# Raw weight slots by quarters, handed on in a circle, and a new order of products and sums in the MLP of a hybrid encoder layer

## The chip, the cores and the metric

The kernel runs on one NeuronCore of a Trainium2 chip. The metric is the device time of one execution in microseconds (us), here the median of three runs. In the profile PE is the matmul engine (its weight loads are PEld), DVE is VectorE, ACT is ScalarE, POOL is GpSimd and SP is the engine that issues most of the transfers.

## What is computed

One layer of a streaming encoder on 512 tokens of width 2048, all in float32: a token mixer, a residual and a layer norm, then the part that the change touches, an MLP with 8192 hidden units.

```python
mix = token_mixer(h, ...)
x = layer_norm(ALPHA * x + g1 * mix, ln1_g, ln1_b)
h = x * (1.0 + sc2) + sh2
ff = jnp.square(jax.nn.relu(h @ w_ff1)) @ w_ff2      # 2048 -> 8192 -> 2048
x = layer_norm(ALPHA * x + g2 * ff, ln2_g, ln2_b)
```

## The kernel before

**Three matmuls for one.** A float32 operand is split into a high part and a low part in the rounded matmul type: `split(h, l, src)` has ACT copy `src` into `h` (L57, the tiles `wh`) and DVE subtract `h` from `src` into `l` (L60, the tiles `wl`). A product is then h·h + l·h + h·l, three matmuls. Most raw weights are loaded by `load` (L127) into the pool `rawp`, four slots of 1 MB under the name `raw`.

**Seven products for eight.** In most of the MLP a unit multiplies a block of weights, cut into quarters a11, a21, a12, a22, with quarters of the activations by Strassen's scheme in Winograd's form. The function `strassen` (L1179) makes seven products of one quarter or one sum of quarters each, named p1 to p7, and eight matrix additions on the weights: s1 = a21 + a22, s2 = s1 + a11, then in place a11 = a11 + a21 and s2 = s2 + a12; each is done in two halves `c` of 128 x 1024 elements. The tiles of s1 and s2 come from four slots (`st` in the first matrix, `s` in the second). Each product is likewise run in two halves: split half c of the quarter into a `wh` and a `wl` (three buffers of each), then the matmuls. The order is p1 (a11), p2 (a12), p6 (s2), p7 (a11 + a21), p5 (s1), p4 (a22), p3 (s2 + a12). Three PSUM areas x, z, v collect the products, and `read` takes each result out of PSUM.

**First matrix.** Block 0 of w_ff1 is done with plain products; then `ff1_unit(b)` runs for blocks 1 to 15, 48 matmuls of 256 columns in a product (L202 to L204). A unit loads four tiles of 1 MB: `lo[c]` holds a11 beside a21, `hi[c]` a12 beside a22. The sums of s are formed behind the two halves of p2 (`late=True`). The inputs t3, n2, n1 and t4 are made on DVE and ACT just before unit 1, from tiles `st` that are read from `hx_d` in runs of 1 KB. What `read` takes out becomes four quarters of the hidden activations (ACT: ReLU and square; DVE: adds). For blocks 0 to 13 seven pieces (three quarters, four sums) are split into tiles `hc` (two slots) and stored to `hc_d`, 512 KB each in runs of 4 KB (`put`, L1090). They stand in a list, `waiting`, and `spread()` runs one of them after each product. Blocks 14 and 15 are stored to `h_d`.

**Second matrix.** `ff2_unit(e, cp, ...)` runs for seven row blocks e and two column pairs cp, 14 units, 24 matmuls of 512 columns in a product (L1374 to L1376). Again four loads of 1 MB. The activations are read back as `hin` (1 MB for each of the seven pieces, in the order of the list `ORDER`), the next e's while the current one's second unit runs. Here the sums of s are formed behind p1. `read` adds each result to `ffa` on DVE; for e > 0 the quadrant (0, 0) goes through an ACT copy `c` and an accumulating transfer that POOL issues. Beside the units run background jobs: `base` (tiles `y`, `lng`, `lnb`) and the gate row g2 (`araw`, `adaz`, and matmuls with `ones` on L1335). The last block e = 7 is done with plain products, followed by the last layer norm.

**What sets the order.** A planner puts each engine's instructions in one fixed order before the run, by its own estimate of durations and by priorities; loads of weights (`w_load`, +2500) and splits and sums (`w_split`, +4000) go ahead of most else. On the chip each engine then works through its list in order, so an instruction that waits holds up all that stand behind it, on SP too. A load is held on SP until its slot's last reader is done.

## Time and profile before

| | us |
|---|---|
| runs | 2266.93, 2272.72, 2273.12; median 2272.72 |
| profiled execution, its own time | 2262.95 |
| its span, first to last instruction | 2261.2 |
| PE busy | 2159.0 (95%) |
| DVE busy | 1873.2 (83%) |
| ACT busy | 1092.9 (48%) |
| granted TensorE clock, mean | 0.987 of full |

The profiled execution's own time lies 1.75 us above its span. Busy time of PE counts pipelined matmuls whose ends are modelled, so a busy PE is not a PE at its peak. In the span the first matrix's units run from 971.8 to 1609.4 us and the second's from 1611.0 to 2160.2 us.

### The profile page before, as it was taken

To read this page: it belongs to the slowest core of one execution; us is meant where nothing else is said; L and a number is where in the kernel's file an instruction comes from. 1 tells how busy PE (TensorE), PEld (TensorE's weight loads), DVE (VectorE), ACT (ScalarE), POOL (GpSimd) and SP (SyncE) were. 2 spreads that over 40 slices of the span, in tenths; PEclk is the share of its full clock that TensorE was granted. 3 is DMA by queue.
4 is the path that set the end of the run, shared out by engine and by line. 5 is a ranking of instruction groups with operands and counts; after the bars stand their busy time and mean duration, and the time that the engine had idled before them with its cause. 6 is when DMAs were issued, how large, how long until landed. Compare 5 with 4: busy or idle time off the path is not lost.

```text
span 2261.2 us, 30621 instructions
## 1 busy us (share of the span) xinstructions
PE 2159.0 (95%) x11947; PEld 1849.2 (82%) x11947; DVE 1873.2 (83%) x2520; ACT 1092.9 (48%) x1570; POOL 44.6 (2%) x55
## 2 busy tenths in 40 slices
PE   6999999988899999999999999999999999999997
PEld 4778887866676787899999999999888887878886
DVE  7886889998776776798778778778699989998788
ACT  3323434458855223666555555555444444444432
POOL 0000000000000000000000000000000000000000
PEclk9999999999999999999999999999999999999999
DMA  8877553264224576745654544553788988796562
GB/s 320 320 292 278 182 216 135 96 208 154 79 84 172 208 282 264 242 142 205 212 187 178 199 183 176 197 187 140 289 303 281 335 276 290 236 343 226 146 235 90
DMA packets 129626, 485.59 MB, mean 215 GB/s; under 512 B 15556, under 2 KB 38468, under 8 KB 88264
## 3 DMA queue, kind: packets, MB, share of 16 engines
q1 hardware_dynamic: 122952, 471.04, 56.9%
q0 software_dynamic: 6528, 12.58, 3.3%
q8 instruction: 94, 1.54, 0.3%
q14 instruction: 52, 0.43, 0.1%
HBM read 392.35 MB, written 78.64 MB: 208 GB/s over the span
## 4 chain that ended last, share of the span: by engine, by line
PE 44%; DVE 32%; DMA 15%; ACT 5%; issue 4%; DVEq 0%; SPq 0%; ACTq 0%
DMA raw<-in_wff_dram 11%; DVE wl L60 10%; PE two L1375 4%; PE two L1376 4%; PE two L1374 4%; DVE st L60 4%; PE mm L210 4%; PE mm L209 4%; PE mm L208 4%; PE mm L197 4%; PE mm L198 4%; PE mm L196 4%; DVE ffa L60 2%; DVE adaz L63 2%; DVE hc L60 2%
## 5 line engine op out<-in xcount | busy, mean ns | idle before, releaser
L57 ACT ACTIVATE wh<-raw 128x1024 fp32r<-128x1024 f32 x332 | 349.5, 1057 | 427.4 <-PE two L1376 137.9
L60 DVE TENSOR_TENSOR wl<-raw,wh 128x1024 fp32r<-128x1024 f32 x332 | 403.1, 1220 | 69.4 <-ACT wh L57 68.9
L1375 PE MATMUL two<-wl,hin 128*128 128x512 f32 x784 | 307.8, 393 | 3.3 <-DVE wl L60 3.0
L1374 PE MATMUL two<-wh,hin 128*128 128x512 f32 x784 | 307.1, 392 | 3.8 <-ACT wh L57 2.1
L1376 PE MATMUL two<-wh,hin 128*128 128x512 f32 x784 | 306.1, 390 | 0.0
L196 PE MATMUL mm<-acts,wh 128*128 128x512 f32 (+1 forms) x568 | 225.5, 400 | 7.3 <-ACT ve L57 3.8
L203 PE MATMUL mm<-acts,wl 128*128 128x256 f32 x720 | 209.4, 291 | 18.4 <-DVE wl L60 18.2
L197 PE MATMUL mm<-acts,wl 128*128 128x512 f32 (+1 forms) x568 | 223.6, 394 | 1.9 <-DVE wl L60 1.7
L198 PE MATMUL mm<-acts,wh 128*128 128x512 f32 (+1 forms) x568 | 223.6, 395 | 0.0
L63 DVE SCALAR_TENSOR_TENSOR adaz<-raw,cols,adaz 128x1024 f32<-128x1024 f32 (+2 forms) x180 | 198.3, 1112 | 17.5 <-DMA raw<-in_adaR_dram 13.4
L202 PE MATMUL mm<-acts,wh 128*128 128x256 f32 x720 | 206.1, 286 | 1.3 <-ACT ev L57 1.3
L204 PE MATMUL mm<-acts,wh 128*128 128x256 f32 x720 | 206.0, 286 | 0.0
L203 PE MATMUL mm<-tx,wl 128*128 128x256 f32 x720 | 203.8, 283 | 0.0
L204 PE MATMUL mm<-tx,wh 128*128 128x256 f32 x720 | 203.3, 282 | 0.0
L202 PE MATMUL mm<-tx,wh 128*128 128x256 f32 x720 | 201.9, 280 | 0.0
L1375 PEld LDWEIGHTS two<-wl,hin 128*128 128x128 f32 x784 | 147.6, 188 | 40.3 <-DVE wl L60 9.2
L1374 PEld LDWEIGHTS two<-wh,hin 128*128 128x128 f32 x784 | 147.5, 188 | 36.0 <-ACT wh L57 3.0
L209 PE MATMUL mm<-wl,acts 128*128 128x512 f32 x448 | 175.0, 391 | 1.2 <-DVE wl L60 1.0
L210 PE MATMUL mm<-wh,acts 128*128 128x512 f32 x448 | 174.7, 390 | 0.0
L208 PE MATMUL mm<-wh,acts 128*128 128x512 f32 x448 | 173.6, 391 | 0.2 <-DVE r L60 0.2
L1376 PEld LDWEIGHTS two<-wh,hin 128*128 128x128 f32 x784 | 147.6, 188 | 30.4
L203 PEld LDWEIGHTS mm<-acts,wl 128*128 128x128 f32 x720 | 140.6, 195 | 24.4 <-DVE wl L60 24.4
(316 smaller groups left out, 4539.1 us busy)
## 6 DMA issues: line engine op xcount, KB each, us to landing
raw<-in_wff_dram SPq DMA_DIRECT2D x128, 1024.0 KB, 6.4
hc_d<-hc SPq DMA_DIRECT2D x98, 512.0 KB, 3.8
hin<-hc_d SPq DMA_DIRECT2D x49, 1024.0 KB, 9.0
raw<-in_adaR_dram SPq DMA_DIRECT2D x48, 1024.0 KB, 5.1
raw<-in_adaS_dram SPq DMA_DIRECT2D x32, 1024.0 KB, 9.0
raw<-in_wo_dram SPq DMA_DIRECT2D x16, 1024.0 KB, 5.0
araw<-in_adaR_dram SPq DMA_DIRECT2D x16, 1024.0 KB, 6.3
raw<-in_wconv_dram SPq DMA_DIRECT2D x12, 1024.0 KB, 4.8
```

The costliest lines, as they stand in the source:

```text
L57: S.activation(o, i, f, **kw)
L60: V.tensor_tensor(o, a, b, op=op)
L196: T.matmul(ps, wh, xh, start=start, stop=False)
L197: T.matmul(ps, wl, xh, start=False, stop=False)
L198: T.matmul(ps, wh, xl, start=False, stop=stop)
L202: T.matmul(ps, wh, xh, start=start, stop=False, skip_group_check=True)
L203: T.matmul(ps, wl, xh, start=False, stop=False, skip_group_check=True)
L204: T.matmul(ps, wh, xl, start=False, stop=stop, skip_group_check=True)
L209: T.matmul(ps, xh, wl, start=False, stop=False)
L1374: T.matmul(ps[:, t], xh, h[:, k], start=first, stop=False, skip_group_check=True)
L1375: T.matmul(ps[:, t], xh, l[:, k], start=False, stop=False, skip_group_check=True)
L1376: T.matmul(ps[:, t], xl, h[:, k], start=False, stop=last, skip_group_check=True)
```

## The change

Two things change in the MLP's units.

Loads: a unit's weights come as eight loads of 512 KB, one for each quarter and half, in the order a22, a21, a11, a12, into eight half slots (four tiles, allocated once for all units). From one unit to the next the slots are handed on: a22 takes the slot that a21 had, a21 that of a11, a11 that of a12, a12 that of a22. In the first matrix a quarter is a slice of 256 columns, so its runs are 1 KB; in the second they are 4 KB.

Order: s1 is formed before anything else, then come p1 (a11), a21 = a21 + a11 in place, p7 (a21), s2 = s1 + a11, p6 (s2), s2 = s2 + a12, p2 (a12), p5 (s1), p4 (a22), p3 (s2). `ORDER` follows, and `spread` takes two pieces after p1, one after p7, none after p6 and p2, one after p5 and p4 and two after p3.

```diff
-    ORDER = ("b11", "b21", "n2", "t3", "n1", "t4", "b22")
+    ORDER = ("b11", "t3", "n2", "b21", "n1", "t4", "b22")
...
-    waiting = []
-
-    def spread(n=1):
+
+    waiting, PIECES = [], dict(p1=2, p7=1, p6=0, p2=0, p5=1, p4=1, p3=2)
+
+    def spread(n):
...
-    def strassen(halves, tile4, widths, operate, read, late=False):
...
-        def product(ps, name, x, start, stop, behind=None):
...
+    slot8, place = [], {}
+
+    def raw_quarters(sources):
+
+        if not slot8:
+            for _ in range(4):
+                r = rawp.tile([128, 2, 1024], F32, name="raw", bufs=4)
+                slot8.extend([r[:, 0], r[:, 1]])
+            place.update(a11=0, a21=1, a12=2, a22=3)
+        else:
+            place.update(a22=place["a21"], a21=place["a11"], a11=place["a12"], a12=place["a22"])
+        w4 = [{}, {}]
+        for name in ("a22", "a21", "a11", "a12"):
+            for c in range(2):
+                src = sources[name][c]
+                w4[c][name] = slot8[2 * place[name] + c].rearrange("p (k n) -> p k n", k=src.shape[1])
+                with prio("w_load"):
+                    nc.sync.dma_start(w4[c][name], src)
+        return w4
+
+    def strassen(w4, tile4, widths, operate, read):
+
+
+        def sums(name, x, y, new=False):
+            for c in range(2):
+                with prio("w_split"):
+                    if new:
+                        w4[c][name] = tile4()
+                    tt(w4[c][name], w4[c][x], w4[c][y], OP.add)
+
+        def product(ps, name, x, start, stop):
...
         x, z, v = yield
+        sums("s1", "a21", "a22", True)
         product(x, "a11", "b11", True, False)
-        if not late:
-            form(0)
-            form(1)
+        sums("a21", "a21", "a11")
         read("p1", x)
-        product(v, "a12", "b21", True, True, form if late else None)
-        for c in range(2):
-            with prio("w_split"):
-                tt(w4[c]["a11"], w4[c]["a11"], w4[c]["a21"], OP.add)
+        product(z, "a21", "t3", True, False)
+        sums("s2", "s1", "a11", True)
+        read("p7", z)
+        product(x, "s2", "n2", False, False)
+        sums("s2", "s2", "a12")
+        read("p6", x)
+        product(v, "a12", "b21", True, True)
         read("p2", v)
-        product(x, "s2", "n2", False, False)
...
         product(x, "s1", "n1", False, False)
         read("p5", x)
         product(z, "a22", "t4", False, True)
...
     def ff1_unit(b):
...
+        w4 = raw_quarters({f"a{i + 1}{j + 1}": [A["wff1"][b][2 * j + c][:, :, 256 * i:256 * i + 256] for c in range(2)]
+                           for i in range(2) for j in range(2)})
...
-            spread()
+            spread(PIECES[name])
...
     def ff2_unit(e, cp, h_in, h_next):
...
+        w4 = raw_quarters({f"a{i + 1}{j + 1}": [A["wff2"][e][2 * cp + i][c][:, 2 * j:2 * j + 2] for c in range(2)]
+                           for i in range(2) for j in range(2)})
```

## Rows read from the trace of the kernel before

**Rows 1.** The page's part 1 (busy us of each engine, its share of the span, instructions) and, from its part 5, the groups of the split's ScalarE step (line, operation, tiles, shapes, count; busy us and mean ns of one; idle us before and what ended it).

```profile
PE 2159.0 (95%) x11947; PEld 1849.2 (82%) x11947; DVE 1873.2 (83%) x2520; ACT 1092.9 (48%) x1570; POOL 44.6 (2%) x55
...
L57 ACT ACTIVATE wh<-raw 128x1024 fp32r<-128x1024 f32 x332 | 349.5, 1057 | 427.4 <-PE two L1376 137.9
```

**Rows 2.** Busy time by stretch of the span: the 15 units of the first MLP matrix, the 14 units of the second, and the first 12 of those 14. Columns: stretch and its length, busy us (and instructions) of PE, its weight loads, DVE, ACT, POOL; granted TensorE clock, mean busy share of the DMA engines, GB/s.

```profile
971.80:1609.40 637.60, 618.16 (x5040) 611.68 (x5040) 508.48 (x531) 367.95 (x479) 0.00 (x0) 0.99 0.52 187
...
1611.00:2160.20 549.20, 543.78 (x2361) 443.08 (x2362) 497.70 (x455) 242.33 (x234) 29.89 (x25) 1.00 0.80 274
...
1611.00:2081.80 470.80, 465.38 (x2021) 379.21 (x2021) 430.95 (x394) 204.65 (x197) 25.09 (x21) 1.00 0.85 293
```

**Rows 3.** The columns of rows 2, one row for a unit of the first matrix (units 1, 4, 5 and 12 of 15). A row counts an instruction at an edge twice, so 338 stands for 336 matmuls.

```profile
971.80:1013.60 41.80, 40.81 (x337) 40.53 (x337) 37.71 (x39) 26.05 (x37) 0.00 (x0) 1.00 0.45 152
...
1096.80:1144.00 47.20, 43.81 (x339) 43.20 (x338) 37.36 (x40) 26.88 (x36) 0.00 (x0) 0.93 0.49 179
1144.00:1184.30 40.30, 40.30 (x338) 40.30 (x338) 33.16 (x36) 24.16 (x32) 0.00 (x0) 1.00 0.54 197
...
1438.10:1485.40 47.30, 43.70 (x339) 43.09 (x338) 36.24 (x39) 26.68 (x36) 0.00 (x0) 0.93 0.45 167
```

**Rows 4.** The columns of rows 2, one row for a unit of the second matrix (the first, third, fifth, seventh, eighth and tenth of 14).

```profile
1611.00:1654.70 43.70, 40.77 (x169) 32.76 (x169) 35.97 (x35) 17.16 (x17) 0.00 (x0) 0.96 0.85 319
...
1693.10:1731.20 38.10, 38.10 (x169) 31.54 (x169) 36.26 (x32) 17.61 (x17) 2.53 (x2) 1.00 0.94 325
...
1769.60:1808.10 38.50, 38.48 (x169) 31.38 (x168) 38.20 (x35) 16.71 (x16) 2.40 (x2) 1.00 0.95 324
...
1846.50:1886.50 40.00, 38.84 (x169) 31.31 (x169) 35.01 (x36) 16.70 (x16) 2.40 (x2) 1.00 0.80 245
1886.50:1926.80 40.30, 40.15 (x173) 32.22 (x172) 36.40 (x34) 17.72 (x17) 3.35 (x3) 1.00 0.88 307
...
1965.00:2005.40 40.40, 39.32 (x169) 31.17 (x168) 37.07 (x33) 16.70 (x16) 2.40 (x2) 1.00 0.81 277
```

**Rows 5.** Who waited for whom between 971.8 and 1609.4 us. Columns: waiting engine, tile and line, what it waited for, us in total, times, longest us.

```profile
DVE st L60 <- DMA raw<-in_wff_dram: 81.5, 28, 5.1
...
ACT hc L57 <- DMA hc_d<-hc: 41.0, 32, 4.8
...
PE mm L203 <- DVE wl L60: 18.2, 25, 2.8
```

**Rows 6.** DVE in order of time, from unit 7 of the first matrix to unit 8 (which begins at 1267.2 us). Columns: start us, us, engine, line, operation, tiles, shapes; in brackets the idle time before and what ended it.

```profile
1252.05 1.23 DVE L60 TENSOR_TENSOR st<-raw 128x1024 f32<-128x1024 f32 x1 [3.32 <-DMA raw<-in_wff_dram]
...
1254.45 2.35 DVE L60 TENSOR_TENSOR wl<-raw,wh 128x1024 fp32r<-128x1024 f32 x2
...
1265.06 1.23 DVE L60 TENSOR_TENSOR st<-raw 128x1024 f32<-128x1024 f32 x1 [3.45 <-DMA raw<-in_wff_dram]
```

**Rows 7.** SP's transfers in order of time, same stretch (x2: two issued in the time given).

```profile
1242.52 2.67 SPq L127 DMA_DIRECT2D raw<-in_wff_dram  x2
...
1255.69 1.47 SPq L127 DMA_DIRECT2D raw<-in_wff_dram  x2
```

**Rows 8.** Groups of DVE instructions between 971.8 and 1609.4 us. Columns: line, operation, tiles, shapes and count; busy us and mean ns of one; idle us before them and what ended it.

```profile
L60 DVE TENSOR_TENSOR wl<-raw,wh 128x1024 fp32r<-128x1024 f32 x120 | 145.4, 1219 | 7.8 <-ACT wh L57 7.8
L60 DVE TENSOR_TENSOR wl<-st,wh 128x1024 fp32r<-128x1024 f32 x90 | 109.9, 1222 | 24.5 <-ACT wh L57 24.5
L60 DVE TENSOR_TENSOR st<-st,raw 128x1024 f32<-128x1024 f32 x60 | 73.2, 1221 | 0.5
L60 DVE TENSOR_TENSOR hc<-ev,hc 128x512 fp32r<-128x512 f32 x98 | 66.1, 687 | 12.5 <-ACT hc L57 12.5
L60 DVE TENSOR_TENSOR raw<-raw 128x1024 f32<-128x1024 f32 x30 | 36.6, 1220 | 0.0
L60 DVE TENSOR_TENSOR st<-raw 128x1024 f32<-128x1024 f32 x29 | 35.5, 1226 | 81.5 <-DMA raw<-in_wff_dram 81.5
```

**Rows 9.** Transfers by tiles over the whole span. Columns: tiles, issuing queue, operation and count, KB each, median us from issue to landing.

```profile
raw<-in_wff_dram SPq DMA_DIRECT2D x128, 1024.0 KB, 6.4
hc_d<-hc SPq DMA_DIRECT2D x98, 512.0 KB, 3.8
...
st<-hx_d SPq DMA_DIRECT2D x8, 512.0 KB, 5.9
```

**Rows 10.** Groups of PE instructions between 1611 and 2160.2 us (columns as in rows 8).

```profile
L1335 PE MATMUL two<-adaz,ones 128*128 128x512 f32 x8 | 3.8, 592 | 0.0
```

**Rows 11.** PE in order of time at the start of the first unit of the second matrix, two of the starts after an idle time.

```profile
1624.86 0.50 PE L1374 MATMUL two<-wh,hin 128*128 128x512 f32 x1 [2.12 <-ACT wh L57]
1626.16 0.50 PE L1375 MATMUL two<-wl,hin 128*128 128x512 f32 x1 [0.81 <-DVE wl L60]
```

**Rows 12.** DVE in order of time in the same stretch as rows 11.

```profile
1613.62 0.43 DVE L67 TENSOR_SCALAR lng<-lng 128x512 f32<-128x512 f32 x1 [1.90 <-DMA lng<-in_ln1g_dram]
...
1616.35 1.22 DVE L60 TENSOR_TENSOR s<-raw 128x1024 f32<-128x1024 f32 x1
...
1624.89 2.35 DVE L60 TENSOR_TENSOR wl<-s,wh 128x1024 fp32r<-128x1024 f32 x2
```

**Rows 13.** DVE in order of time in the tenth unit of the second matrix.

```profile
1994.61 1.22 DVE L60 TENSOR_TENSOR s<-raw 128x1024 f32<-128x1024 f32 x1 [2.84 <-DMA raw<-in_wff_dram]
```

**Rows 14.** DVE in order of time in the seventh unit of the second matrix.

```profile
1860.18 0.69 DVE L60 TENSOR_TENSOR y<-y,lng 128x512 f32<-128x512 f32 x1 [2.37 <-DMA y<-xn_d]
```

More of the change, by code (lines that the diff above doesn't have):

```diff
@@ L1177, in trunk_kernel @@
             parts(t4, a)
-    def strassen(halves, tile4, widths, operate, read, late=False):
-        w4 = [dict(zip(("a11", "a21", "a12", "a22"), h)) for h in halves]
-        def form(c):
-            with prio("w_split"):
-                tt(new_s(c, "s1"), w4[c]["a21"], w4[c]["a22"], OP.add)
-                tt(new_s(c, "s2"), w4[c]["s1"], w4[c]["a11"], OP.add)
-        def new_s(c, name):
-            w4[c][name] = tile4()
-            return w4[c][name]
-        def product(ps, name, x, start, stop, behind=None):
+    slot8, place = [], {}
[23 more added lines that the diff above has]
+        def product(ps, name, x, start, stop):
             for c in range(2):
@@ L1198, in product @@
                     split(h, l, w4[c][name])
-                if behind is not None:
-                    behind(c)
                 operate(ps, h, l, x, c, start and c == 0, stop and c == 1)
         x, z, v = yield
+        sums("s1", "a21", "a22", True)
         product(x, "a11", "b11", True, False)
-        if not late:
-            form(0)
-            form(1)
+        sums("a21", "a21", "a11")
         read("p1", x)
-        product(v, "a12", "b21", True, True, form if late else None)
-        for c in range(2):
-            with prio("w_split"):
-                tt(w4[c]["a11"], w4[c]["a11"], w4[c]["a21"], OP.add)
-        read("p2", v)
-        product(x, "s2", "n2", False, False)
-        for c in range(2):
-            with prio("w_split"):
-                tt(w4[c]["s2"], w4[c]["s2"], w4[c]["a12"], OP.add)
-        read("p6", x)
-        product(z, "a11", "t3", True, False)
-        read("p7", z)
+        product(z, "a21", "t3", True, False)
[5 more added lines that the diff above has]
+        product(v, "a12", "b21", True, True)
+        read("p2", v)
         product(x, "s1", "n1", False, False)
@@ L1235, in ff1_unit @@
     def ff1_unit(b):
-        lo, hi = [None] * 2, [None] * 2
-        for c in range(2):
-            lo[c] = load(A["wff1"][b][c], [128, 4, 512])
-            hi[c] = load(A["wff1"][b][2 + c], [128, 4, 512])
-        halves = [(lo[c][:, :, 0:256], lo[c][:, :, 256:512], hi[c][:, :, 0:256], hi[c][:, :, 256:512])
-                  for c in range(2)]
+        w4 = raw_quarters({f"a{i + 1}{j + 1}": [A["wff1"][b][2 * j + c][:, :, 256 * i:256 * i + 256] for c in range(2)]
+                           for i in range(2) for j in range(2)})
         inputs = dict(b11=b11, b21=b21, n2=n2, t3=t3, n1=n1, t4=t4, b22=b22)
@@ L1283, in read @@
                 sums_done(b, [part[q] for q in QUARTERS])
-            spread()
-        run(strassen(halves, st_tile, [128, 4, 256], operate, read, True), (bank(), bank(), bank("sa")))
+            spread(PIECES[name])
+        run(strassen(w4, st_tile, [128, 4, 256], operate, read), (bank(), bank(), bank("sa")))
     for b in range(1, 16):
@@ L1357, in ff2_unit @@
     def ff2_unit(e, cp, h_in, h_next):
-        wa, wb = [None] * 2, [None] * 2
-        for c in range(2):
-            wa[c] = load(A["wff2"][e][2 * cp][c], [128, 4, 512])
-            wb[c] = load(A["wff2"][e][2 * cp + 1][c], [128, 4, 512])
-        halves = [(wa[c][:, 0:2], wb[c][:, 0:2], wa[c][:, 2:4], wb[c][:, 2:4]) for c in range(2)]
+        w4 = raw_quarters({f"a{i + 1}{j + 1}": [A["wff2"][e][2 * cp + i][c][:, 2 * j:2 * j + 2] for c in range(2)]
+                           for i in range(2) for j in range(2)})
         def operate(ps, h, l, name, c, start, stop):
@@ L1398, in read @@
                 tick()
-        run(strassen(halves, lambda: HC.tile([128, 2, 512], F32, name="s", bufs=4), [128, 2, 512], operate, read),
+        run(strassen(w4, lambda: HC.tile([128, 2, 512], F32, name="s", bufs=4), [128, 2, 512], operate, read),
             [two_banks() for _ in range(3)])
```

## The prediction

> **What bounds the kernel now.** I read the page's part 1 first: PE is busy 95% of the span, DVE 83% [rows 1]. Such an average hides where PE waits, so the next view is busy time by stretch [rows 2]. The two stretches that the change touches are the 15 Strassen units of the first MLP matrix, 637.6 us, and the 14 of the second, 549.2 us; the rest of the span, some 1,074 us, it leaves alone. Cut by unit, the first stretch shows what a unit takes when nothing stalls: unit 5 takes 40.3 us with PE busy in all of it, which is 5.76 us for each of its seven products and 2.88 us for each half of a product [rows 3]. Fifteen such units are 604.5 us, so the stretch holds 33.1 us that are not products at full rate. Unit 1 has 1.5 us of these; units 4 and 12 have 7 us each, and there the granted clock is 0.93, so after the stall PE ran for a while at the lower of its two levels (1.2 and 2.4 GHz). In the second stretch a unit without stall takes 38.1 us [rows 4]; 14 of them are 533.4 us, and 15.8 us are over.
>
> The table of waits names the cause in the first stretch [rows 5]: DVE waits 81.5 us for raw weights, 28 times, and PE waits 18.2 us for DVE's low parts (wl). PE never waits for a transfer itself; the two are tied by DVE's order. Unit 7 into unit 8 shows it [rows 6, 7]. SP issues two loads for unit 8 at 1242.5 to 1245.2 us. DVE has come to s1 of unit 8, which needs both, and stands 3.32 us until 1252.05; behind it in DVE's queue are the low parts for unit 7's p4, which run only at 1254.45, and PE starves. The other two loads are issued at 1255.7 and DVE stands for them until 1265.06, two microseconds before unit 8 begins; then the sums and splits of that unit come late too. The loads are late because of slots: a 1 MB tile holds a11 beside a21, or a12 beside a22, so it comes free only when p7 (fourth product) or p4 (sixth) has been split.
>
> **The change part by part.**
>
> Slots. In the new order a21's quarter is last read by p7's split (second product), a11's by s2 (third), a12's by p2's split (fourth), a22's by p4's split (sixth), and each goes to the quarter that the next unit wants first. Three wh and wl buffers let a half's split run up to two halves (5.8 us) before PE wants it. So a22 and a21 are issued some 28 us or more before the next unit begins, a11 about 23 us, and a12, which is first read after the next unit's p6 split, about 20 us before that. A load took 1252.05 - 1245.2 = 6.9 us, or 1265.06 - 1257.2 = 7.9 us after its pair was issued [rows 6, 7]. All four are covered, and the waits of both kinds go. The tightest is a11, because a21 + a11 is a sum that DVE's queue may hold early: s1 must come before it and s1's tile comes free with p5's split, 20 to 23 us into the unit, while a11's loads leave at 14 and 17 us (p2 starts at 17.3, and its halves' splits end some 3 us before PE wants them). That is 3 to 9 us against 7 to 8, so DVE may still stand for a few us; the splits run up to 3 us ahead of PE. I bound this at 0 to 1 us a unit and take 0.2, since s1 and the splits of p4 stand between.
>
> DVE's work. Eight sums of 1.22 us a unit before (120 in 15 units [rows 8]) and eight after; 14 splits in both; nothing is gained or lost in sum. Unit 5 uses DVE 33.2 of 40.3 us, so the new order fits when the loads are there. The deadlines move: four sums (s1 and the new a21, 4.9 us) must now precede the second product, where four had to precede the third. They are hidden in products 5 to 7 of the unit before, where DVE has only six splits. That cover is missing in the first unit of each stretch. In unit 1 DVE is busy 37.7 of 41.8 us [rows 3], so I keep its 1.5 us and add 2, between 0 and 4.9.
>
> Pieces. The seven pieces a unit that go out as hc are the same; they come 2, 1, 0, 0, 1, 1, 2 in place of one a product. Bounds 0 to 1 us a unit (worked out with the rivals); it is in the 0.2 above.
>
> Loads. Eight of 512 KB in place of four of 1 MB, in runs of 1 KB (first matrix) or 4 KB (second). The nearest rows: the store of hc, 512 KB in 4 KB runs, lands in 3.8 us; the load of st, 512 KB in 1 KB runs, in 5.9; a 1 MB weight load in 6.4 [rows 9]. Per byte that is 1.19 to 1.84 times a 1 MB load. The transfer engines are busy 0.52 of the first stretch and 0.80 of the second [rows 2]. In the first, weights are 63 of 119 MB, so 1.84 times makes it about 0.75: hidden. In the second I take the 1.19, as the runs are the store's: weights are 58.7 of 150 MB, 0.31 of the 0.80, and it becomes 0.86: hidden. SP issues four more transfers a unit; a pair took it 1.47 us, and 2.67 where it had to wait [rows 7]. What waits behind a load that SP holds for its slot are the hc stores, and behind these ACT's next hc split.
>
> A rule speaks against this part. The Trainium skill, "DMA: Bandwidth & Descriptors", section on the anatomy of one DMA, gives 2.0 us plus bytes over 436 GB/s for each transfer, which is 4.4 us for 1 MB and 3.2 us for half; its section on bandwidth says to batch to 1 MiB or more. By that an estimate would be 45% more per byte, 0.14 of share in the second stretch: the units at 0.94, 0.95 and 0.88 [rows 4] would pass 1.0 by 0.08, 0.09 and 0.02, some 7 us, and the sum would be 7 us less. The trace lies partly with it: the hc store's 3.8 us is near its 3.2, the weight load's 6.4 well above its 4.4, so by the rows halving costs less.
>
> Second matrix. Of the 15.8 us, some 3.8 are g2's matmuls (units 8 and 14), which stay [rows 10]. Unit 1's 5.6 us: PE stalls at the third product, 1624.86 and 1626.16 [rows 11], since DVE stood for lng until 1613.62 and made the first s only at 1616.35 and its low parts at 1624.89 [rows 12]. That is no load of weights; the tiles of s lie where the first stretch's inputs lay. Now s1 is wanted for the second product, 5.4 us sooner, while only two sums of s are needed first instead of four: I keep 5.6, between 0 and 11. Unit 10's 2.3 us [rows 4] are a load (DVE stands 2.84 us [rows 13]) and go. Unit 7's 1.9 us come from y and lng [rows 14]: half. Of the remaining 2.2, half.
>
> Sum. First stretch: 33.1 - 1.5 - 2 - 14 x 0.2 = 26.8 us gained. Second: 2.3 + 1.0 + 1.1 = 4.4. Together 31.2. On the profiled execution's own time, 2262.95 us (span 2261.2), that is 2231.8. The runs' median is 2272.72, 9.8 above that execution; the forecast is for the median, 2272.7 - 31.2 = **2241.5 us**. Best case of the bounds: 33.1 + 15.8 - 3.8 = 45.1 us, 2227.6. Worst: unit 1 loses 2.9 more, the other 28 units 0.8 to 1 us, the second stretch's start 5.6; that eats all 31 us.
>
> **The rivals.**
>
> A new wait takes part of it (2248 to 2265). Five pieces (2, 2, 1) fall in p3, p1 and p7, 17.3 us, and there are two hc tiles. A tile's round is DVE's 0.69 us [rows 8], ACT's half of the split, which I put at the same, and issue and landing, 4.1: 5.5 us, so two tiles need 13.7 us for five. It fits, but with the longest wait of 4.8 [rows 5] a round is 10.3 and five need 25.7, 8 us too many, of which the splits' lead covers all but 1 or 2 us. At 1 us in 14 units, 2255.
>
> The change does not do what it says (2266 to 2279): DVE is the real limit, and its waits only fill time that it would lose elsewhere. For it: DVE is busy 80% of the first stretch and 91% of the second [rows 2]. Against: unit 5 has the same DVE work and no stall.
>
> The chain s1, a21 + a11, split ends on the path of every unit (slower). Four sums, then ACT's 1.06 [rows 1] and DVE's low part, with one split between: about 6.9 us from s1's start to p7's first low part, against 5.76 for p1. If s1 is begun with the first product, a unit loses 1.1 us, and 29 units lose what is gained above; if 2 us later, 3.1 us, and 29 units lose 90 for 31 gained: 2331. So it decides for slower from the unit's start on. For it: now s1's second half ends 1 us before unit 8 begins [rows 6]. Against: that was the late load.
>
> Transfers bind in the second matrix (slower). Its first 12 units have a share of 0.85 [rows 2]. At the 1.84 of the 1 KB load it would be 0.85 + 0.31 x 0.84 = 1.11 over 470.8 us: 52 us lost, 31 gained, 2293. It decides from about 1.7 times per byte. Against: 1.19 for 4 KB runs.
>
> **How the numbers follow.** Most of the gain kept (2228 to 2248): 0.60. Partly (2248 to 2265): 0.19. No change: 0.09. Slower: 0.12, the chain 0.07 and the transfers 0.05. A difference of 0.3%, 6.8 us, is about what a measurement of this kernel can tell. So faster 0.79, same 0.09, slower 0.12. The range 2228 to 2265 holds the first two, 0.79.
>
> **What would show it.** Right: DVE's wait for raw weights falls from 81.5 to under 15 us in the first stretch, PE's wait for wl from 18.2 to under 6; the stretch takes 605 to 615 us with the granted clock at 1.00 throughout; in DVE's order s1 and a21 + a11 of a unit stand among the low parts of the unit before; the second stretch takes 540 to 547 us with a transfer share under 0.90. Wrong: waits for raw weights that stay, now at the a21 sum; PE waits at p7 in every unit; more than 41 us of ACT waiting for hc stores with PE waiting behind; a first unit of the second matrix of over 49 us.

## The result, and the profile after

The changed kernel took 2240.39 us (median of 4 runs, 2238.53 to 2243.67) against 2272.56 us of the kernel before beside it (4 runs, 2266.93 to 2273.12): ratio 0.9867, 95% interval 0.9851 to 0.9884. The forecast was 2241.5 us in a range of 2228 to 2265. On a second occasion it took 2241.95 against 2266.64 us, ratio 0.9888 (0.9864 to 0.9912). So the gain is 32.2 us the first time and 24.7 us the second, 1.1 to 1.3%. One of the four runs of e6_unit1_old (below) took 8226.18 us and is left out of its time. The profiled execution's own time is 2243.67 us, its span 2241.9; that of before was 2262.95 and 2261.2.

Part 1 of the page of after; the line of before is in [rows 1]:

```profile
PE 2151.6 (96%) x11947; PEld 1848.8 (82%) x11947; DVE 1880.8 (84%) x2520; ACT 1096.3 (49%) x1570; POOL 44.6 (2%) x55
```

PE's busy time is 7.4 us less with the same matmuls, which is not the change's doing: a second profile of the kernel before (e0_before, below) has 2151.7 us. DVE has the same 2520 instructions. Next the stretches and some units, with the columns of [rows 2] and [rows 3, 4]: the first matrix (978.0 to 1590.8), its first unit and its other 14; the second matrix (from 1591.5) and its first three units.

```profile
978.00:1590.80 612.80, 607.57 (x5040) 606.29 (x5040) 517.35 (x531) 370.14 (x479) 0.00 (x0) 1.00 0.57 194
978.00:1026.40 48.40, 43.17 (x337) 42.07 (x338) 43.72 (x46) 27.96 (x40) 0.00 (x0) 0.96 0.49 169
1026.40:1590.80 564.40, 564.40 (x4706) 564.22 (x4704) 473.63 (x485) 342.18 (x439) 0.00 (x0) 1.00 0.58 196
1591.50:2140.60 549.10, 541.74 (x2361) 444.48 (x2362) 494.25 (x451) 243.54 (x235) 30.22 (x26) 0.99 0.82 274
1591.50:1638.00 46.50, 41.40 (x169) 33.19 (x170) 38.89 (x37) 18.32 (x18) 0.34 (x1) 0.93 0.85 306
1638.00:1678.80 40.80, 39.05 (x169) 31.39 (x168) 31.69 (x31) 18.51 (x18) 0.00 (x0) 1.00 0.83 285
1678.80:1716.90 38.10, 38.10 (x169) 31.42 (x168) 35.93 (x32) 17.62 (x17) 2.53 (x2) 1.00 0.79 253
```

The first matrix fell from 637.6 to 612.8 us. Units 2 to 15 take 564.4 us and PE is busy in all 564.40 of them: 40.31 each, no stall left. Everything that is over sits in the first unit, 48.4 us where before it took 41.8 [rows 3]. The second matrix stands at 549.1 us, where it stood before (549.2 [rows 2]): its first unit rose from 43.7 [rows 4] to 46.5, its second from 38.4 to 40.8, and the others gave back what these two cost.

Who waited for whom in the first matrix (columns of [rows 5]; a total, times, longest):

```profile
ACT wh L57 <- PE mm L204: 151.9, 120, 2.7
DVE wl L60 <- ACT wh L57: 75.9, 85, 3.0
...
ACT hc L57 <- DMA hc_d<-hc: 28.7, 20, 2.6
...
PE mm L203 <- DVE wl L60: 2.8, 2, 1.7
```

The row that led in before, DVE for raw weights with 81.5 us [rows 5], has no successor: DVE doesn't wait for a weight load there at all. PE's wait for low parts fell from 18.2 to 2.8 us, twice instead of 25 times. The two waits now at the top, ACT for PE and DVE for ACT, are those of engines that run ahead. The transfers (columns of [rows 9]):

```profile
raw<-in_wff_dram SPq DMA_DIRECT2D x232, 512.0 KB, 4.6
```

Eight loads of 512 KB landed in 4.6 us each (median), where 1 MB took 6.4. The mean share of the transfer engines went from 0.52 to 0.57 and from 0.80 to 0.82.

Two profiles of one kernel differ too. The kernel before, profiled once more (e0_before below), and the changed kernel's second profile (e4_after_again) give two pairs: first matrix 637.6 and 634.2 us before, 612.8 and 612.6 after; second matrix 549.2 and 550.6 before, 549.1 and 550.8 after. And the part ahead of the MLP, which the change doesn't touch, took 968.7 to 978.0 us in the 14 profiles of this case. The stretches by themselves therefore give 21 to 25 us, and the 7 us or more on top in the first timing are within what that untouched part moves from one execution to the next.

### The profile page after: what moved, and what is told of

The parts are those of the page before. It is cut to its first block, busy times and chain, and to the rows that moved or that the text cites. A ratio compares the mean times of both kernels' runs of the same rounds, so it can differ in the third digit from the quotient of the medians.

```text
span 2241.9 us, 30919 instructions
## 1 busy us (share of the span) xinstructions
PE 2151.6 (96%) x11947; PEld 1848.8 (82%) x11947; DVE 1880.8 (84%) x2520; ACT 1096.3 (49%) x1570; POOL 44.6 (2%) x55
## 4 chain that ended last, share of the span: by engine, by line
PE 68%; DVE 20%; ACT 5%; DMA 4%; issue 3%; SPq 0%; DVEq 0%; ACTq 0%
PE mm L203 8%; PE mm L204 7%; PE mm L202 7%; PE two L1380 5%; PE two L1381 5%; PE two L1379 5%; DVE wl L60 5%; PE mm L197 4%; PE mm L198 3%; PE mm L196 3%; PE mm L210 3%; PE mm L209 3%; PE mm L208 3%; DVE ffa L60 2%; DVE adaz L63 2%
## 5 line engine op out<-in xcount | busy, mean ns | idle before, releaser
L203 PE MATMUL mm<-acts,wl 128*128 128x256 f32 x720 | 204.5, 284 | 1.7 <-DVE wl L60 1.7
L57 ACT ACTIVATE wh<-st 128x1024 fp32r<-128x1024 f32 x90 | 95.4, 1060 | 105.5 <-PE mm L204 83.9
```

The source lines that it names most:

```text
L57: S.activation(o, i, f, **kw)
L203: T.matmul(ps, wl, xh, start=False, stop=False, skip_group_check=True)
```

## The experiments

The table of stretches is what to follow: first matrix, second matrix, in us.

| kernel | order | slots | first | second |
|---|---|---|---|---|
| before | old | four of 1 MB | 637.6 | 549.2 |
| e0_before | old | four of 1 MB | 634.2 | 550.6 |
| e1_order_only | new | four of 1 MB | 622.4 | 555.4 |
| e2_slots_only | old | eight, circle | 610.6 | 579.4 |
| e3_own_slots | new | eight, no circle | 616.6 | 582.4 |
| after | new | eight, circle | 612.8 | 549.1 |
| e4_after_again | new | eight, circle | 612.6 | 550.8 |
| e5_old_order_own_circle | old | eight, its own circle | 610.3 | 585.7 |
| e6_unit1_old | new but one unit | eight, circle | 612.6 | 549.4 |
| e7_base_later | new, y work later | eight, circle | 612.7 | 544.8 |
| e8_old_order_bg_pool | old | eight, circle | 609.7 | 598.4 |
| e9_pieces_one | as after, told below | eight, circle | 612.8 | 554.0 |
| e10_old_order_bg_last | old, no background | eight, circle | 610.5 | 544.2 |
| e11_best | old, then new, y work later | eight, circle | 611.0 | 545.1 |

**One part alone.** First the kernel before as it is, and the two halves of the change.

> The kernel before once more, unchanged, for a second profile of it. The stretch ahead of the first matrix (0 to 971.8 us in the first profile of before, 978.0 us in that of after) has the same instructions in the same order in both kernels. If its length differs from execution to execution, it comes out anywhere from 970 to 985 us here. If the first profile was typical, it is 970 to 973 us. In either case the 15 units of the first matrix should again take 634 to 642 us, with units of 42 to 47 us, and the 14 of the second 547 to 552 us.

One execution took 2259.48 us. Its two stretches are as expected, though single units of the first came out at 40.3 to 46.6 us:

```profile
970.00:1604.20 634.20, 614.69 (x5040) 607.89 (x5040) 507.99 (x531) 367.11 (x479) 0.00 (x0) 1.00 0.52 188
1605.80:2156.40 550.60, 543.85 (x2361) 443.19 (x2362) 497.44 (x455) 242.38 (x234) 29.88 (x25) 1.00 0.80 273
```

For the order alone, the new order and pieces stayed and the loads of both matrices went back to four tiles of 1 MB (the first matrix is shown):

```diff
-        w4 = raw_quarters({...})
+            lo[c] = load(A["wff1"][b][c], [128, 4, 512])
+            hi[c] = load(A["wff1"][b][2 + c], [128, 4, 512])
+        w4 = [dict(a11=lo[c][:, :, 0:256], a21=lo[c][:, :, 256:512], a12=hi[c][:, :, 0:256], a22=hi[c][:, :, 256:512])
+              for c in range(2)]
```

> Only the new order of products, sums and pieces; the loads are the four 1 MB tiles of before. My theory (late slots cause the waits): the second pair of loads still waits for p4's split, the sixth product in both orders, so DVE's wait for raw weights in the first matrix stays above 25 us, units of the first matrix stay at 41 to 43 us, and the kernel takes 2252 to 2272 us. Rival (the order alone, with the sums in other places, relieves DVE): units fall to 40.3 to 40.6 us, DVE's wait for raw falls under 10 us, and the kernel takes 2236 to 2246 us, as after.

Measured: 2256.61 us, ratio 0.9958 (0.9941 to 0.9976). The stretches, and the wait for weights in the first:

```profile
970.80:1593.20 622.40, 611.52 (x5040) 607.84 (x5040) 512.26 (x531) 364.29 (x479) 0.00 (x0) 0.99 0.55 191
1593.90:2149.30 555.40, 543.99 (x2361) 442.85 (x2361) 492.43 (x450) 243.31 (x235) 30.16 (x26) 0.99 0.79 271
```

```profile
DVE st L60 <- DMA raw<-in_wff_dram: 23.5, 14, 2.1
```

The order alone takes DVE's wait from 81.5 to 23.5 us and 12 to 15 us out of the first matrix, though the slots are as coarse as before; the sums that need the late loads come at other places, which I take to be the reason, but no run parts it from the rest. It costs 5 to 6 us in the second. The time lies in my theory's range, but its least wait was 25 us, and it had no gain for the order; the rival's under 10 us and 2236 to 2246 us are farther off.

For the slots alone, the circle stayed, and order, pieces and `ORDER` were those of before:

```diff
-    ORDER = ("b11", "t3", "n2", "b21", "n1", "t4", "b22")
+    ORDER = ("b11", "b21", "n2", "t3", "n1", "t4", "b22")
...
-    waiting, PIECES = [], dict(p1=2, p7=1, p6=0, p2=0, p5=1, p4=1, p3=2)
+    waiting, PIECES = [], dict(p1=1, p7=1, p6=1, p2=1, p5=1, p4=1, p3=1)
...
```

> Only the eight quarter slots and the circle; products, sums and pieces in the order of before. My theory: slots come free after the second, third and fourth product and after the sixth, so weights land before they are wanted, DVE's wait for raw in the first matrix falls under 15 us and units 2 to 15 take 40.3 to 40.8 us; the first unit takes about 42 us as before, where after takes 48.4; the kernel takes 2232 to 2244 us. Rival (the order carries the gain): four sums behind p2 still crowd DVE, units stay at 41 to 43 us, the kernel takes 2252 to 2270 us.

Measured: 2267.98 us, ratio 1.0010 (0.9992 to 1.0028). This expectation fell: I had the slots carry nearly all of the gain, and on the clock they carry none. The stretches say why:

```profile
975.70:1586.30 610.60, 606.16 (x5040) 605.08 (x5040) 518.35 (x531) 369.47 (x479) 0.00 (x0) 1.00 0.58 195
1587.90:2167.30 579.40, 555.79 (x2361) 448.11 (x2362) 498.85 (x455) 242.29 (x234) 29.89 (x25) 0.98 0.78 260
```

In the first matrix the expectation nearly holds: 610.6 us, 2 better than the change, with the second unit at 43.8 us and 13 units at the rate without stall. DVE's wait for raw weights is 16.7 us there, above the 15 that I had, yet PE waits only 0.9 us for low parts: what counts is how much of such a wait reaches PE. But the second matrix lost 29 to 30 us, and the clock there is 0.98.

For the circle, the new order kept its quarter loads but each quarter went to its own slot again:

```diff
-            place.update(a22=place["a21"], a21=place["a11"], a11=place["a12"], a12=place["a22"])
+            pass
```

> After with one thing undone: each quarter is loaded into its own slot again instead of being handed on. a22 then waits for p4's split (28 us into a unit), though s1 wants it first. My theory: DVE stands at s1 for 2 to 4 us in each half of each unit, 40 to 100 us in all in the first matrix, units take 41 to 44 us and the kernel 2250 to 2285 us. Rival (half-size slots and the order are enough, the circle adds nothing): units of 40.3 us, the kernel within 0.3% of after, 2234 to 2247 us.

Measured: 2274.58 us, ratio 1.0046 (1.0028 to 1.0064).

```profile
973.70:1590.30 616.60, 609.66 (x5040) 606.89 (x5040) 510.69 (x531) 361.50 (x479) 0.00 (x0) 1.00 0.58 193
1591.00:2173.40 582.40, 553.82 (x2361) 442.95 (x2362) 494.31 (x451) 243.40 (x235) 30.22 (x26) 0.99 0.77 258
```

Two waits of its second stretch:

```profile
ACT wh L57 <- DVE raw L60: 61.6, 17, 7.2
...
DVE s L60 <- DMA raw<-in_wff_dram: 34.8, 12, 5.7
```

In the second matrix the circle's worth is direct: without it s1 waits for its two quarters (34.8 us), and ACT stands 61.6 us for the sum a21 + a11 behind it. In the first matrix my theory missed: DVE's wait for raw weights is 17.3 us and not 40 to 100, and the stretch is only 3.8 us longer than with the circle. So in the second matrix each of these three kernels, with a part of the change left out, loses 5 to 33 us, and only all parts together are even.

**Why the slots alone lose in the second matrix.** My first idea was that the circle frees slots in the order of the new products only. I gave the old order a circle of its own:

```diff
-            place.update(a22=place["a21"], a21=place["a11"], a11=place["a12"], a12=place["a22"])
+            place.update(a11=place["a21"], a12=place["a12"], a21=place["a11"], a22=place["a22"])
...
-        for name in ("a22", "a21", "a11", "a12"):
+        for name in ("a11", "a12", "a21", "a22"):
```

> The old order of products and sums, one piece of hc each, the eight slots of quarters, but handed on in the order in which the OLD order lets go of them: loads a11, a12, a21, a22; the new a11 goes to the slot of the old a21, a12 to that of a12, a21 to that of a11, a22 to that of a22. Theory 1 (the slots alone gave nothing because the circle of the change frees its slots in the order of the new products only, so that in the old order a load waits at the head of SP's queue and holds those behind it): the second matrix falls from 579 us (slots with the change's circle, old order) to 547 to 555, the first stays at 610 to 613, and the time is within 0.4% of the changed kernel. Theory 2 (the reordering itself is needed, because s1 wants a21 and a22 before the third product and their slots come free late in the old order whatever the map): the second matrix stays over 565 us and the ratio to before is 0.995 to 1.003.

Measured: 2272.61 us, ratio 1.0026 (1.0008 to 1.0044), second matrix 585.7 us. Theory 1 fell, and theory 2's numbers came out. That its reason, s1's late slots, was the cause is not shown by that: DVE does wait for weights at the sums, but two more rows of that stretch point to the background.

```profile
DVE s L60 <- DMA raw<-in_wff_dram: 18.4, 5, 6.5
DVE adaz L63 <- DMA araw<-in_adaR_dram: 16.1, 8, 3.4
...
DVE y L60 <- DMA y<-xn_d: 10.9, 3, 5.8
```

DVE stands for `araw` and `y`, the loads of the background jobs, 27.0 us in all. The next idea was that SP's queue holds them behind raw loads. So they went to POOL's queue, in the kernel with the slots alone:

```diff
-            nc.sync.dma_start(r, src)
+            (nc.gpsimd if tag == "araw" else nc.sync).dma_start(r, src)
...
-            nc.sync.dma_start(y, xn_d[t][:, cs_])
+            nc.gpsimd.dma_start(y, xn_d[t][:, cs_])
```

> The old order with the slots and the change's circle (the kernel whose second matrix took 579 us), with the background loads of the second matrix (araw of the gate's sums, and y) issued on POOL's queue instead of SP's. Theory 1 (the 30 us lost there come of SP's queue: raw loads that wait for a slot hold araw and y behind them, DVE stands at the late araw or y ahead of the next split, and PE's clock falls): waits of DVE for araw and y go from 18.2 us to under 6, the second matrix to 548 to 560 us, the time to 2240 to 2253. Theory 2 (DVE's own sums are crowded in the old order with one slot each, whatever the background does): the second matrix stays at 570 us or over, and DVE's waits for raw and wh, not for araw, stand ahead of PE's stalls. A wash in between (560 to 570) would say that both carry part.

Measured: 2287.82 us, ratio 1.0078 (1.0053 to 1.0104), second matrix 598.4 us. Theory 1 missed: it got worse, with DVE's waits for the background up from 18.2 to 43.7 us. Theory 2's number came out (570 us or over), but not its reason, as the waits for weights are almost gone.

```profile
DVE adaz L63 <- DMA araw<-in_adaR_dram: 28.0, 8, 7.7
...
DVE y L60 <- DMA y<-xn_d: 15.7, 4, 7.8
...
DVE s L60 <- DMA raw<-in_wff_dram: 2.4, 1, 2.4
```

The timeline of the slots-alone kernel then showed what I had overlooked, DVE first and SP's load below it:

```profile
2006.68 1.28 DVE L63 SCALAR_TENSOR_TENSOR adaz<-araw,cols,adaz 128x1024 f32<-128x1024 f32 x1
2007.88 1.22 DVE L60 TENSOR_TENSOR wl<-s,wh 128x1024 fp32r<-128x1024 f32 x1
2009.13 1.23 DVE L60 TENSOR_TENSOR s<-s,raw 128x1024 f32<-128x1024 f32 x1
2010.27 1.22 DVE L60 TENSOR_TENSOR wl<-s,wh 128x1024 fp32r<-128x1024 f32 x1
2011.52 1.23 DVE L60 TENSOR_TENSOR s<-s,raw 128x1024 f32<-128x1024 f32 x1
2017.29 1.28 DVE L63 SCALAR_TENSOR_TENSOR adaz<-araw,cols,adaz 128x1024 f32<-128x1024 f32 x1 [4.54 <-DMA araw<-in_adaR_dram]
```

```profile
2007.99 0.33 SPq L127 DMA_DIRECT2D araw<-in_adaR_dram  x1
```

The two sums over one `araw` end at 2007.96, and the load of the next is issued at 2007.99. There is one `araw` buffer; the load waits for the sums and not for SP's queue. DVE's fixed order puts only four instructions, 4.8 us of work, before the next sum, and that sum starts 9.3 us after the issue (the median time to landing is 8.1 us here, 6.3 in before, 7.7 in after, over the loads whose landing the trace shows). DVE stands 4.54 us, and the low parts behind it starve PE for 4.0. By the same timelines, 6 of the 15 gaps between `araw` pairs hold under 7 us of DVE work in this kernel, 6 of 15 in before too, and none in after, where the least is 8.1. So the old order was as tight before, but the load came sooner then, and DVE waited 5.2 us for `araw` in all; with the quarter slots 16.4. In after it is 1.1. Why this load takes longer beside the quarter slots stays open.

The test: hold all of the background on DVE behind the last unit (`mark[0]` is the last sum of that unit).

```diff
-            if e > 0 and name in ("p5", "p4", "p3"):
-                tick()
...
-    while bg:
-        tick()
+    with tc.issue_after(mark[0].ins):
+        while bg:
+            tick()
```

> The old order with the slots and the change's circle, and all of the background of the second matrix (the gate's sums over araw, lng, lnb, y) held on DVE behind the last sum of the last unit, so that the 14 units run without it; the end of the kernel pays for that with the whole background (32 sums of 1.28 us and 32 of 0.68 us on DVE, 63 us, and their loads), so only the second stretch counts. Theory 1 (what the 30 us there come from is the background: DVE takes its instructions in order and stands at an araw or y whose load is late on its queue): the 14 units fall from 579 us to 538 to 550. Theory 2 (DVE's own sums come too late in the old order once each quarter has a slot of its own, background or not): they stay at 560 us or over, with PE's stalls at p7, p5 and p4 behind sums that wait for raw.

Measured: 2360.57 us in one execution, with a tail of 226.6 us, as intended. The 14 units:

```profile
1587.70:2131.90 544.20, 537.90 (x2352) 440.26 (x2352) 444.15 (x383) 238.45 (x230) 28.93 (x24) 1.00 0.71 231
```

544.2 us instead of 579.4: theory 1's number came out. DVE still waited 18.1 us for weights in that stretch, as with the background (18.4), yet PE's waits fell from 25.0 to 7.8 us. What this run can't part is the background's waits from its mere 55 us of DVE time, as it takes both out; a second `araw` buffer, which would part them, was not run. Nor does any run show what the background costs the kernel before or the changed one.

**The first units.** The 8.1 us that the change leaves in the first matrix, and what is over in the second, are mostly in the first units. The changed kernel as it is was run beside these kernels:

> The changed kernel as it is, on the same chip as the three kernels beside it, to compare them with. Ratio to the kernel before 0.985 to 0.989; all units of the first matrix but the first at 40.31 us, the first at 46 to 49; first two units of the second matrix 46.5 and 40.8 us. If the first units differ from that by more than 1 us, their stalls are a matter of one execution and not of the order.

Measured: 2241.95 us, with the ratio told above; first units of 48.2 and 47.8 us, second unit of the second matrix 39.4. Its first units differ from the first profile by 0.2, 1.3 and 1.4 us, but the first two of the second matrix together take 87.3 us in both. So the stalls belong to the order, and only their shares in the second matrix to the execution. The old order in the first unit alone (the arguments that are added choose the old order and form the sums behind the halves of p2):

```diff
-        run(strassen(w4, st_tile, [128, 4, 256], operate, read), ...
+        run(strassen(w4, st_tile, [128, 4, 256], operate, read, b == 1, True), ...
```

> The changed kernel with the first unit of the first matrix alone in the old order (s1 and s2 formed within the second product). Theory 1 (the unit's 8.0 us over 40.31 come of four sums that the new order puts on DVE ahead of p6, while DVE still makes the combined inputs): the unit falls to 42 to 43 us, the second rises to at most 42, 3 to 6 us are saved against the changed kernel. Theory 2 (the inputs are owed in any order and the stall only moves into the second unit): the first two units together stay at 88 us or over, the time within 2 us of the changed kernel.

```profile
976.40:1024.50 48.10, 43.09 (x336) 42.81 (x337) 43.05 (x45) 27.17 (x39) 0.00 (x0) 0.93 0.48 166
1024.50:1064.80 40.30, 40.30 (x338) 40.30 (x337) 36.32 (x39) 25.68 (x34) 0.00 (x0) 1.00 0.67 235
```

Measured: 2242.34 us (the middle one of 2238.96, 2242.34 and 2243.62) against 2241.95 of the changed kernel beside it. Theory 2's numbers hold, the two units take 88.4 us as after (88.7), but the stall did not move into the second unit. One piece per product instead:

```diff
-    waiting, PIECES = [], dict(p1=2, p7=1, p6=0, p2=0, p5=1, p4=1, p3=2)
+    waiting, PIECES = [], dict(p1=1, p7=1, p6=1, p2=1, p5=1, p4=1, p3=1)
```

> The changed kernel with one piece of the previous block's hc work per product (1,1,1,1,1,1,1) instead of 2,1,0,0,1,1,2. Theory 1 (the pieces are arranged for the new order: without it the four early sums meet an ev sum or an hc piece within p6 and p2): units 2 to 15 of the first matrix rise from 40.31 to 40.5 to 41.5 us, 3 to 15 us lost. Theory 2 (the slots carry the gain and the pieces fit anyway): units 2 to 15 stay at 40.31 to 40.4; only the first unit moves, down by 1 to 3 us, since block 0's pieces no longer fall two at a time on a DVE that is behind.

```profile
1583.80:2137.80 554.00, 543.06 (x2361) 444.03 (x2362) 494.06 (x451) 243.51 (x235) 30.21 (x26) 0.99 0.81 271
```

Measured: 2245.46 us, ratio 0.9892 (0.9876 to 0.9909), first matrix 612.8 us. Neither theory is tested by this. In the two traces every engine's instructions, SP's transfers included, stand in the same order as in after, one by one: as far as the traces show, the planner makes the same program of both arrangements of the pieces. So the new arrangement has no effect in the changed kernel, and the run is a third timing and profile of it: 23.8 us gained, and a second matrix of 554.0 us, 3 to 5 longer than in the other two profiles, with waits of DVE for `y` of 10.6 us (7.5 in after). By their stretches the three profiles of the changed kernel are 18 to 25 us better than the two of the kernel before.

In the second matrix DVE stood for lng and lnb ahead of s1. The rows of after, DVE first and then PE at the start of the second product:

```profile
1594.55 0.43 DVE L67 TENSOR_SCALAR lng<-lng 128x512 f32<-128x512 f32 x1 [4.25 <-DMA lng<-in_ln1g_dram]
1596.04 0.43 DVE L67 TENSOR_SCALAR lnb<-lnb 128x512 f32<-128x512 f32 x1 [1.06 <-DMA lnb<-in_ln1b_dram]
1596.38 2.35 DVE L60 TENSOR_TENSOR s<-raw 128x1024 f32<-128x1024 f32 x2
...
1602.06 2.35 DVE L60 TENSOR_TENSOR wl<-raw,wh 128x1024 fp32r<-128x1024 f32 x2
```

```profile
1601.01 0.79 PE L1379 MATMUL two<-wh,hin 128*128 128x512 f32 x1 [3.61 <-ACT wh L57]
1603.28 0.79 PE L1379 MATMUL two<-wh,hin 128*128 128x512 f32 x1 [1.48 <-ACT wh L57]
```

Their work was put behind the sums of a later unit (`mark[0]` is the last sum that the program had written by then, and lng's scaling came to stand in the sixth unit):

```diff
-        ts(g_, g_, ALPHA, None, OP.mult)
-        ts(b_, b_, ALPHA, None, OP.mult)
+        with tc.issue_after(mark[0].ins):
+            ts(g_, g_, ALPHA, None, OP.mult), ts(b_, b_, ALPHA, None, OP.mult)
```

> The changed kernel with the two scalings of lng and lnb, and with them the y work that hangs on them, held on DVE behind the sums of the first unit of the second matrix's second stretch of hidden units (the place where the program writes them); nothing else moves on any engine but SP's loads and stores of y. Theory 1 (DVE stands 5.3 us at lng and lnb ahead of s1, PE waits behind that and its clock falls; and 5.1 us at y in the second unit): first unit of the second matrix 38.5 to 41 us instead of 46.5, second 38.1 to 38.5 instead of 40.8, 6 to 10 us saved, second stretch 539 to 544. Theory 2 (s1 would wait for the raw quarters or the banks anyway): under 2 us saved. Theory 3 (the y work only moves its stalls into later units): the two units gain, later ones lose 3 us or more of it.

Measured: 2237.12 us, ratio 0.9875 (0.9846 to 0.9905); PE, ACT and POOL have the same order as in after.

```profile
1587.70:2132.50 544.80, 540.42 (x2361) 444.13 (x2362) 492.32 (x450) 243.20 (x235) 30.20 (x26) 1.00 0.82 276
1587.70:1631.70 44.00, 40.55 (x169) 32.67 (x170) 34.75 (x30) 17.97 (x18) 0.32 (x1) 0.96 0.89 324
1631.70:1670.10 38.40, 38.40 (x169) 31.55 (x168) 31.59 (x29) 18.51 (x18) 0.00 (x0) 1.00 0.74 271
```

The second unit fell to 38.4 as expected. The first two units take 82.4 us, 4.8 less than in all three profiles of the changed kernel, and the stretch is 4 to 9 us shorter than in these. But the first unit stopped at 44.0, above the 38.5 to 41. ACT shows the rest:

```profile
1593.61 1.02 ACT L57 ACTIVATE ffa<-two 128x1024 f32<-128x1024 f32 x1 [5.31 <-PE two L1381]
1594.53 1.99 ACT L57 ACTIVATE wh<-raw 128x1024 fp32r<-128x1024 f32 x2
```

The first split of the new a21 was ready on DVE at 1591 and stands on ACT behind the read-out of p1, which waits 5.31 us for p1 to end. That read-out is ahead of the split in ACT's list in after as well.

**A version of both.** The edits of e7_base_later and e9_pieces_one, and the old order in all units of the first matrix, where one piece per product belongs to it:

```diff
-        run(strassen(w4, st_tile, [128, 4, 256], operate, read), ...
+        run(strassen(w4, st_tile, [128, 4, 256], operate, read, True, True), ...
```

> Eight slots and the change's circle, the old order in all units of the first matrix with one piece of hc per product (first stretch 610.6 and 609.7 us in the two kernels that had it, 612.8 in the changed kernel), the new order in the second matrix, with the y work behind the first sums as in the kernel with base later (second stretch 544.8 us). Theory 1 (the two gains are in different stretches and add): first stretch 609 to 611, second 543 to 547, time 2231 to 2238, ratio to before 0.983 to 0.988. Theory 2 (the debt of the first two units returns, or the new order's first unit of the second matrix finds its quarters later behind a last unit in the old order): first stretch over 612 or second over 548, and the time is 2238 to 2246.

```profile
968.70:1579.70 611.00, 609.03 (x5040) 608.00 (x5040) 519.16 (x532) 369.85 (x479) 0.00 (x0) 0.99 0.58 195
1580.40:2125.50 545.10, 540.82 (x2361) 443.83 (x2362) 492.32 (x450) 243.16 (x235) 30.16 (x26) 1.00 0.83 276
```

Measured: 2235.55 us (2228.84 to 2242.62), ratio 0.9877 (0.9846 to 0.9907). The stretches add as theory 1 has it; the second unit of the first matrix takes 44.2 us, as it took 43.8 in e2_slots_only. By its two stretches it is 6 to 11 us better than the three profiles of the change; by the runs neither it nor e7_base_later can be told from the change, since all the intervals overlap.

## Why the prediction was right, point by point

**The cause, right.** Fifteen units with 33.1 us over, from loads that came late to DVE's queue: the wait is gone, and 14 units run at the 40.31 us that unit 5 showed. I kept 0.2 us a unit for a21 + a11 and the pieces; it is 0.0, and the pieces' new arrangement changed nothing at all (e9). But I had the whole gain come of the slots and their handing on. The order alone, with the old slots, gives 12 to 15 us of it (e1), the slots alone give 24 to 27 (e2), and the handing on is worth only 3.8 us in this stretch (e3).

**The first unit, mis-sized.** I kept 1.5 + 2 us, at most 6.4. It is 8.1. I counted four sums without cover. DVE's groups in that unit (columns of [rows 8]):

```profile
L60 DVE TENSOR_TENSOR wl<-raw,wh 128x1024 fp32r<-128x1024 f32 x9 | 10.9, 1217 | 1.5 <-ACT wh L57 1.5
...
L60 DVE TENSOR_TENSOR hc<-ev,hc 128x512 fp32r<-128x512 f32 x9 | 6.1, 683 | 0.0
```

These are nine low parts of raw quarters and nine `hc` steps, where before there were seven and four: 46 DVE instructions and 43.7 us busy in 48.4. Before, DVE was busy 37.7 of 41.8 us, the same nine tenths, so the counts of a longer unit don't say what made it longer. The order of that one unit is not it (e6). Nor is it the new order by itself, which e3 has without the handing on:

```profile
973.70:1015.60 41.90, 41.87 (x336) 41.88 (x337) 39.23 (x40) 26.49 (x37) 0.00 (x0) 0.96 0.54 176
```

There the first two units take 85.2 us together, with the old order in the whole matrix 86.3 to 86.8 (e2, e11), after 88.7, and with the new order on the old slots 89.3 (e1). Before, they took 82.3. What the difference is made of is not settled.

**Sum of the first stretch:** 26.8 us forecast, 24.8 by one pair of profiles, 21.6 by the other.

**The second matrix, wrong in its terms.** I forecast 4.4 us gained and a stretch of 540 to 547; it is 0 and 549.1. Unit 10's 2.3 us went, as said, and unit 7's 1.9 went whole, where I had half. But the first unit, kept at 5.6 in bounds of 0 to 11, came to 8.4, and the second, which I had at nothing, to 2.7. The forecast named the way (s1 is wanted 5.4 us sooner and lng stands before it) and then took the middle. The rows said more: DVE had stood at lng until 1613.62 [rows 12] and PE felt it at the third product; with s1 wanted one product sooner it is felt at the second, and for longer (3.61 and 1.48 us). e7 shows this part to be worth 4.8 us in the two units. g2's term holds: its eight matmuls take 3.8 us as before.

**The total, right partly by chance.** The stretches give 18 to 25 us and not 31.2. The first timing's 32.2 agrees with the forecast; the second, 24.7, and the third, 23.8 (e9), agree with the stretches. The untouched part varies by up to 9.3 us from profile to profile, enough for the difference, but that it made it is not shown, as only one execution of each set of runs has a profile. All of this is well inside the range.

**What I had not seen at all:** that in the second matrix the slots need the order. In the sum the slots made the gain and the order only had to fit. In the first matrix that is so (e2: 610.6 with the old order). In the second the old order with the new slots loses 30 us, and without the background that loss is gone (e10). Of DVE's waits the one for `araw` grew most with the slots, from 5.2 to 16.4 us; the forecast does not name it. No rival had it either, although DVE at 91% of that stretch [rows 2] stood there for it.

**The transfers.** Forecast 0.86 of share in the second stretch, measured 0.82; the rival that they bind is out. But the term behind the 0.86 was mis-sized. In the second matrix (1612 to 2130 us) the weight loads landed so, before and after:

```profile
raw<-in_wff_dram SPq DMA_DIRECT2D x52, 1024.0 KB, 7.1
```

```profile
raw<-in_wff_dram SPq DMA_DIRECT2D x100, 512.0 KB, 5.7
```

That is 1.6 times per byte and not 1.19, and by the prediction's own sum it would have made a share of 0.99. The share rose by 0.02 only: here the time to landing did not say how long the transfer engines are busy. The Trainium skill, "DMA: Bandwidth & Descriptors", section on bandwidth, says to batch to 1 MiB or more; it gives this for transfers that GpSimd issues, while these loads are issued by SP. By the prediction's estimate, from the formula of the Trainium skill, "DMA: Bandwidth & Descriptors", section on the anatomy of one DMA, which is for GpSimd's path too, some 7 us would have been lost in units that pass a share of 1.0. The trace doesn't bear that out here: the share rose by 0.02 to 0.05, and units 4 and 5 of the second matrix run at 38.08 us.

**The rival of the pieces** (ACT waiting for the stores of `hc`, 2248 to 2265) is out: that wait fell from 41.0 [rows 5] to 28.7 us.

**The other two rivals.** The chain s1, a21 + a11, split was to cost each unit 1 us or more; with 14 units at 40.31 us it is out. That DVE is the real limit is out in the first matrix. The second did as this rival has it, the same time with other stalls; but e7, with the same DVE instructions in another order, shows that there too it is their order that counts, for 4.8 us.

## What to carry to other kernels

A slot that holds two things is held by the one that is read last. Cutting it into parts, with an order of reading that suits them, took a whole class of waits away here, though each transfer became half as large. What the handing on of the parts adds differs by stretch: 3.8 us in one matrix, 28 to 33 in the other. Such a change has to be judged in every stretch that uses it, with the background jobs of that stretch: on an engine that takes its instructions in a fixed order, a job with a single buffer stalls everything behind it once its load takes longer than the work placed between two of its steps. The first unit of a pipelined loop is worth a sum of its own: here the first units hold most of what the forecast missed. And what a planner makes of an edit is to be read in the trace: one edit here left every engine's order as it was.

## What the runs showed that I had not expected

- A load of 1 MB (`araw`) landed in 6.3 us (median; 5.7 and 5.9 in e0_before and e1_order_only) beside four 1 MB weight loads a unit, and in 8.1 beside eight of 512 KB in the old order, 7.7 in the new (7.2 to 8.2 in the others that had them beside it), with the mean share of the transfer engines hardly changed (0.80, 0.78, 0.82).
- Issued from POOL's queue instead of SP's, the same loads landed in 8.2 us (median; up to 13.1), no sooner than from SP (8.1), and each issue took POOL 0.53 to 1.08 us where SP took 0.33.
- The part ahead of the MLP took 968.7 to 978.0 us in different executions, a spread of 9.3 us, more than several of the effects studied here; stretches of one profile tell small effects apart that the total time can't.
